# Two-layer decoder trunk on one core: VectorE in place of GpSimd for the two-operand SBUF arithmetic of layer 0's attention, with a new order of work

## The chip, the cores and the metric

The kernel runs on one core of a Trainium2 chip. A core has five engines that matter here: TensorE (PE in the profile; PEld is its weight load), VectorE (DVE), ScalarE (ACT), GpSimd (POOL) and SyncE (SP), which issues all transfers. Each engine works through its own list of instructions in order; semaphores hold an instruction back until what it reads is there. The metric is the device time of one launch in microseconds, lower is better.

## The reference, cut to what matters

`x` is 256 tokens by 1024 features in float32. Layer 0 is native sparse attention, layer 1 dilated window attention, each with a conditioned norm in front, an output projection, a gated residual add behind, and one norm at the end.

```
h = rms_norm(x, g) * (1 + scale) + shift            # shift, scale, gate: silu(c) @ w_ada + b_ada
u = h @ w_in                                        # q, k_c v_c k_s v_s k_w v_w, z, gate logits
k_cmp, v_cmp = compress(k_c), compress(v_c)         # 15 blocks of 32 tokens, two small matmuls each
o_cmp = softmax(q k_cmp) v_cmp
o_slc = softmax(rope(q) rope(k_s)) v_s              # 4 blocks of 64 tokens, top 16: all visible ones
o_win = softmax(rope(q) rope(k_w)) v_w              # window 512: all earlier tokens
o = g0 * o_cmp + g1 * o_slc + g2 * o_win
x = x + gate * ((o * silu(z)) @ w_out)
...                                                 # layer 1: 16 heads in three (window, dilation) groups
out = rms_norm(x)
```

## The kernel before, in words

Activations lie with tokens or features on the 128 partitions, always whole in SBUF. Weights stream in from memory once, in pieces of 256 KB to 512 KB (tile `raw`). Float32 products are made from a split: a weight piece `raw` is copied to a rounded `wh`, and the rest `wl = raw - wh` is computed (`split`, line 445); activations are split in the same way into `hH`/`hL` (in the attention `hl`, `kl`, and `a` for the operands of later products). A product of two split operands takes three matmuls, `wh*hH + wh*hL + wl*hH`. Every 128 x 512 weight piece so costs a copy and a subtraction before TensorE may use it, and both have two SBUF operands or one.

The program falls into stages, which the code calls phases: 0 the norm of layer 0 and the first part of its input projection, accumulated over 8 slices k of the features in eight banks of PSUM (`lin` three, `s` two, `o` and `t`); 1 the rest of that projection and the whole attention of layer 0; 2 its output projection; 3 and 4 layer 1's projections and attention, half the heads each; 5 layer 1's weighing of the groups, its z gate and its output projection.

In phase 1 there are, beside the matmuls: the splits of the weights that are left of `w_in`; rotary embedding (`rope`, line 696: products of PSUM with a table, then a sum of two SBUF tiles, `t1 + t2`); the splits of q and k (`q_stack`, `k_stack`); the sum with the position table and the probabilities of the compressed branch (`cmp_blocks`, `cmp_probs`); per pair of heads `pair0` (line 940): scores in PSUM, a masked maximum on VectorE (`pt<-pss,ct`), exponentials on ScalarE, a scaling of each 128-row piece of probabilities (`pt<-pt,sm`), transposes on TensorE (`pst<-ct,pt`), their copies to SBUF (`pT<-pst`) and the product with v (`pso<-pT,v`); and the gating of each pair by z and its split (`w<-w,a`, `a<-w,a`).

Nothing is issued in the order in which it is written. Each operation is recorded with its operands (`Order.add`, line 127) and with the engines that may run it: "SV" for a copy, "VG" or "GV" for a sum or difference, "GVS" for the scaling of probabilities. `Order.schedule` (line 193) then fixes one list for each engine: it walks through a planned time with a table of instruction costs, takes on each engine the operation that can start first, breaks ties by a priority (the place in the text plus the group's number in `SHIFT`), and hands an operation with a choice of engines to the one on which it would end first, the cost weighted by the table `W` (one number for each engine and phase). `EARLY` moves the transfers of a group forward or back in SyncE's list. All instructions are therefore issued from one line, 335, and the profile's groups are told apart by their tiles.

What the change touches is the rule in `add` (lines 157 to 164). In the phase whose number is `SPLIT`, an operation that VectorE may share with another engine loses VectorE if it has two wide SBUF operands (`two`) or is a copy or a scaling from SBUF to SBUF (`one`); otherwise it loses GpSimd. In every other phase a choice between VectorE and GpSimd always goes to VectorE. With `SPLIT = 1` the sums and differences of two SBUF tiles in phase 1 so run on GpSimd, the copies from SBUF to SBUF there on ScalarE, and the copies out of PSUM on VectorE or ScalarE.

## Time and profile before

| | us |
|---|---|
| median of 3 runs | 353.34 (350.19 to 354.21) |
| profiled execution, device time | 351.29 |
| its span, first to last instruction | 349.5 |
| TensorE busy | 331.9 (95%) |
| VectorE busy | 241.2 (69%), 699 instructions |
| ScalarE busy | 231.5 (66%) |
| GpSimd busy | 62.3 (18%), 79 instructions |

The span lies 1.8 us under the profiled execution's own time, which lies 2.05 us under the median. A matmul counts as busy from its start to a modelled end, and matmuls overlap, so TensorE's busy time is a cover of the span and not its load. A row of a timeline gives the start, the time covered, the engine, the operation with its tiles, and in brackets the idle time before it with the instruction that ended it. In groups, `x112 | 75.2, 708 | 30.9` is 112 instructions, 75.2 us covered by them, 708 ns the mean of one from start to end, and 30.9 us of idle time in front of them. Means are longer than busy time divided by the count, since the end of one instruction overlaps the start of the next.

### The profile page before, as it was taken

To read this page: it belongs to the slowest core of one execution; us is meant where nothing else is said; L and a number is where in the kernel's file an instruction comes from. 1 tells how busy PE (TensorE), PEld (TensorE's weight loads), DVE (VectorE), ACT (ScalarE), POOL (GpSimd) and SP (SyncE) were. 2 spreads that over 40 slices of the span, in tenths; PEclk is the share of its full clock that TensorE was granted. 3 is DMA by queue.
4 is the path that set the end of the run, shared out by engine and by line. 5 is a ranking of instruction groups with operands and counts; after the bars stand their busy time and mean duration, and the time that the engine had idled before them with its cause. 6 is when DMAs were issued, how large, how long until landed. Compare 5 with 4: busy or idle time off the path is not lost.

```text
span 349.5 us, 6498 instructions
## 1 busy us (share of the span) xinstructions
PE 331.9 (95%) x2217; PEld 264.5 (76%) x2217; DVE 241.2 (69%) x699; ACT 231.5 (66%) x618; POOL 62.3 (18%) x79
## 2 busy tenths in 40 slices
PE   8698999899999999999999799999999999999991
PEld 7485778787956688766886577787887889799881
DVE  1536255666987687868669799946788449597864
ACT  4736245575876998997348765787468788456614
POOL 1000000699721572015400200000000000000000
PEclk9998999999999999999999999999999999999997
DMA  7999996743979941618963974943556125145003
GB/s 234 338 362 355 351 360 190 203 154 102 380 245 356 383 166 62 241 39 317 361 221 106 338 245 121 342 150 113 181 179 190 53 81 167 56 127 175 1 0 120
DMA packets 45168, 71.35 MB, mean 204 GB/s; under 512 B 4712, under 2 KB 22352, under 8 KB 45136
## 3 DMA queue, kind: packets, MB, share of 16 engines
q1 hardware_dynamic: 45136, 70.94, 61.2%
q8 instruction: 17, 0.28, 0.3%
q14 instruction: 15, 0.12, 0.1%
HBM read 69.88 MB, written 1.05 MB: 203 GB/s over the span
## 4 chain that ended last, share of the span: by engine, by line
PE 78%; ACT 5%; DVE 4%; DMA 4%; POOL 4%; issue 2%; SPq 1%; ACTq 0%; POOLq 0%; DVEq 0%
PE pslin L335 50%; PE pst L335 13%; PE pss L335 9%; PE pso L335 6%; DMA raw<-in_nsa_w_in_dram 3%; ACT a L335 2%; DMA vec<-in_ada_b_dram 1%; ACT wh L335 1%; SPq L335 1%; POOL wl L335 1%; DVE t L335 1%; DVE a L335 1%; ACT w L335 1%; POOL sm L335 1%; DVE x L335 1%
## 5 line engine op out<-in xcount | busy, mean ns | idle before, releaser
L335 DVE TENSOR_TENSOR wl<-raw,wh 128x512 fp32r<-128x512 f32 (+2 forms) x128 | 82.5, 683 | 31.9 <-ACT wh L335 25.8
L335 ACT ACTIVATE wh<-raw 128x512 fp32r<-128x512 f32 (+3 forms) x144 | 78.3, 592 | 38.6 <-DMA raw<-in_nsa_w_in_dram 9.3
L335 PE MATMUL pslin<-wh,hH 128*128 128x512 f32 (+1 forms) x136 | 54.5, 405 | 3.1 <-ACT hH L335 3.1
L335 PE MATMUL pslin<-wl,hH 128*128 128x512 f32 (+1 forms) x136 | 53.9, 401 | 0.7 <-DVE wl L335 0.6
L335 PE MATMUL pslin<-wh,hL 128*128 128x512 f32 (+1 forms) x136 | 54.3, 400 | 0.0
L335 ACT ACTIVATE pt<-pt,sm 128x128 f32<-128x128 f32 (+1 forms) x128 | 51.3, 443 | 1.5 <-DVE sm L335 1.3
L335 DVE CUSTOM_DVE_ANT_0 pt<-pss,ct 128x256 f32<-128x256 f32 (+1 forms) x96 | 30.6, 351 | 12.3 <-PE pss L335 9.1
L335 POOL TENSOR_TENSOR sm<-sm,mhalf 128x1 f32<-128x1 f32 x6 | 4.9, 816 | 181.2 <-DVE sm L335 171.2
L335 POOL TENSOR_TENSOR wl<-raw,wh 128x256 fp32r<-128x256 f32 (+2 forms) x24 | 23.9, 1015 | 63.7 <-ACT wh L335 63.6
L335 PEld LDWEIGHTS pslin<-wh,hH 128*128 128x128 f32 x136 | 25.8, 191 | 9.5 <-ACT hH L335 3.7
L335 PE MATMUL pslin<-hH,wh 128*128 128x256 f32 x112 | 31.9, 290 | 1.1 <-DVE t L335 1.1
L335 PE MATMUL pslin<-hH,wl 128*128 128x256 f32 x112 | 31.1, 292 | 0.2 <-POOL wl L335 0.2
L335 PE MATMUL pslin<-hL,wh 128*128 128x256 f32 x112 | 31.1, 288 | 0.0
L335 PE MATMUL pslin<-wh,a 128*128 128x512 f32 x96 | 30.4, 396 | 0.0
L335 PEld LDWEIGHTS pslin<-wl,hH 128*128 128x128 f32 x136 | 25.9, 190 | 5.8 <-DVE wl L335 1.1
L335 PE MATMUL pss<-a,a 128*128 128x256 f32 (+2 forms) x128 | 30.0, 324 | 0.0
L335 PEld LDWEIGHTS pslin<-wh,hL 128*128 128x128 f32 x136 | 26.0, 191 | 4.9 <-issue 0.8
L335 PE MATMUL pst<-ct,pt 128*128 128x128 f32 x144 | 27.2, 280 | 0.0
L335 ACT ACTIVATE a<-pst 128x512 fp32r<-128x512 f32 (+5 forms) x37 | 20.1, 571 | 8.2 <-PE pst L335 8.0
L335 PEld LDWEIGHTS pss<-a,a 128*128 128x128 f32 x128 | 20.8, 190 | 3.0 <-DVE am L335 0.8
L335 PEld LDWEIGHTS pslin<-hH,wh 128*128 128x128 f32 x112 | 21.1, 189 | 2.0 <-ACT wh L335 1.4
L335 PEld LDWEIGHTS pst<-ct,pt 128*128 128x128 f32 x144 | 17.5, 141 | 6.6 <-ACT pt L335 2.0
(206 smaller groups left out, 658.2 us busy)
## 6 DMA issues: line engine op xcount, KB each, us to landing
raw<-in_ada_w_dram SPq DMA_DIRECT2D x32, 512.0 KB, 5.8
raw<-in_dil_w_in_dram SPq DMA_DIRECT2D x32, 512.0 KB, 4.4
a<-in_ada_w_dram SPq DMA_DIRECT2D x32, 256.0 KB, 5.3
raw<-in_nsa_w_in_dram SPq DMA_DIRECT2D x12, 384.0 KB, 4.5
raw<-in_nsa_w_out_dram SPq DMA_DIRECT2D x8, 512.0 KB, 4.9
raw<-in_dil_w_out_dram SPq DMA_DIRECT2D x8, 512.0 KB, 3.6
raw<-in_nsa_w_in_dram SPq DMA_DIRECT2D x8, 320.0 KB, 5.4
raw<-in_nsa_ck_w_dram SPq DMA_DIRECT2D x4, 512.0 KB, 5.4
```

The costliest lines, as they stand in the source:

```text
L335: getattr(self.eng[o["eng"]], name)(*map(self.bind, a), **{n: self.bind(x) for n, x in k.items()})
```

## The change

`SPLIT` becomes -1, which is no phase's number, so the rule of phase 1 is gone: sums and differences of two SBUF tiles go to VectorE in all phases, copies and scalings from SBUF to SBUF may go to VectorE or ScalarE in phase 1 as elsewhere. GpSimd keeps the six small powers of the norms and three fills with zero. `W`, all 62 entries of `SHIFT` and most of `EARLY` (47 entries before, 51 now) have new values, so that the lists of all engines are new in all phases.

```diff
     COLD = 6900.0
-    SPLIT = 1
+    SPLIT = -1
     SWITCH = 140.0
-    W = {"V": [28.3311, 11.5606, 58.1165, 39.0311, 46.0334, 38.3357], "S": [15.1009, 14.1134, 11.5755, 23.4489, 27.2999, 8.7042], "G": [22.0, 22.0, 22.0, 22.0, 22.0, 22.0]}
+    W = {"V": [34.4666, 16.9669, 58.5786, 53.4999, 34.5476, 45.0449], "S": [21.8443, 11.231, 8.2993, 26.6967, 27.0326, 28.6422], "G": [22.0, 22.0, 22.0, 22.0, 22.0, 22.0]}
...
```

By the lists of the two kernels, 66 sums, differences and products of phase 1 move from GpSimd to VectorE (14 of 128 x 512, 12 of 128 x 384, 28 of 128 x 256, 12 of 128 x 128). Over all phases 105 copies and scalings with an SBUF source move from ScalarE to VectorE (44 of them scalings of probabilities, 37 roundings `wh<-raw`), and 64 copies out of PSUM move from VectorE to ScalarE (29 of them `pT<-pst`): now all of `pT`, `qp`, `kl` and the transposed operands `a<-pst` are copied by ScalarE. VectorE's list grows from 699 to 806 instructions. TensorE has the same matmuls in another order.

Three places of the new lists follow; a tile's first number tells buffers of one name apart and its last number is given when it is placed, so the last numbers differ between the lists.

The first is VectorE's list where phase 0 ends and phase 1 begins: `pslin_14` and `pslin_15` hold the first 512 columns (q) of the projection for the two halves of the tokens, `t1_151` and `t2_152` are the rotary products of the first, `qp` and `a4_112` plain copies. Before:

```order
L335 TENSOR_TENSOR wl_103_1528<-raw_50_1366,wh_102_1520 128x512
L335 TENSOR_TENSOR wl_103_1528<-raw_50_1366,wh_102_1520 128x256
L335 COPY qp_115_1572<-pslin_14_1129 128x512
L335 TENSOR_TENSOR t1_151_1579<-pslin_14_1129,ct_68 128x512
L335 TENSOR_TENSOR t2_152_1587<-pslin_14_1129,ct_68 128x8x32
L335 COPY a4_112_1595<-pslin_16_1167 128x512
L335 COPY w1_114_1607<-pso_17_1177 128x128
L335 COPY a4_112_1595<-pso_17_1177 128x512
```

and now:

```order
L335 TENSOR_TENSOR wl_103_1528<-raw_50_1369,wh_102_1521 128x256
L335 TENSOR_TENSOR wl_103_1528<-raw_50_1369,wh_102_1521 128x512
L335 CAST wh_127_1542<-raw_123_1384 128x256
L335 TENSOR_TENSOR wl_128_1547<-raw_123_1384,wh_127_1542 128x256 x2
L335 CAST wh_129_1563<-raw_124_1411 128x256
L335 TENSOR_TENSOR wl_130_1567<-raw_124_1411,wh_129_1563 128x256 x2
L335 TENSOR_TENSOR t1_151_1575<-pslin_14_1128,ct_68 128x512
L335 TENSOR_TENSOR t2_152_1584<-pslin_14_1128,ct_68 128x8x32 x2
L335 TENSOR_TENSOR t1_157_1593<-pslin_15_1130,ct_68 128x512
```

The splits of the next weights (`wl_128`, `wl_130`) have come from GpSimd and stand in front of the rotary products; the plain copies out of PSUM are gone to ScalarE, so both second products `t2_152` follow at once and the bank `pslin_14` is read out sooner after its last matmul.

The second is TensorE's list at the same place: `pslin_163` is the first block of z columns (one `lin` bank, which it takes over from `pslin_14`), `pst_20` the last bank of the projection in phase 0. Before:

```order
L335 MATMUL pso_17_1177<-wl_101_1502,hH_87 128x432
L335 MATMUL pss_18_1189<-wh_102_1520,hH_87 128x512
...
L335 MATMUL pst_20_1204<-hH_87,wh_102_1520 128x256
L335 MATMUL pst_20_1204<-hL_88,wh_102_1520 128x256
L335 MATMUL pst_20_1204<-hH_87,wl_103_1528 128x256
L335 MATMUL pslin_163_1642<-hH_87,wh_127_1541 128x256
L335 MATMUL pslin_163_1642<-hL_88,wh_127_1541 128x256
```

and now:

```order
L335 MATMUL pso_17_1165<-wl_101_1511,hH_87 128x432
L335 MATMUL pslin_163_1598<-hH_87,wh_127_1542 128x256
L335 MATMUL pslin_163_1598<-hL_88,wh_127_1542 128x256
...
L335 MATMUL pslin_163_1598<-hH_87,wl_132_1617 128x256
L335 MATMUL pss_18_1179<-wh_102_1521,hH_87 128x512
L335 MATMUL pss_18_1179<-wh_102_1521,hL_88 128x512
```

The z block now begins before the last slice of the banks `s` and `t`, 18 of its matmuls ahead of them, where it stood behind all of them.

The third is ScalarE's list in phase 0 at the third slice k: `t2_69` is a copy on the way to the slice's scale and shift (`Acol`, `Bcol`), `w1_70` applies them, `hH_87` is what the matmuls wait for. Before:

```order
L335 ACTIVATE t2_69_1248<-pst_68_1233 128x512
L335 ACTIVATE wh_73_1253<-raw_32_1121 128x512
L335 ACTIVATE wh_73_1253<-raw_32_1121 128x256
L335 ACTIVATE wh_76_1267<-raw_33_1124 128x512
L335 ACTIVATE wh_76_1267<-raw_33_1124 128x432
L335 ACTIVATE w1_70_1284<-a4_7_1093,Bcol_86,Acol_85 128x256
L335 ACTIVATE w1_75_1290<-a4_7_1093,Bcol_86,Acol_85 128x256
L335 ACTIVATE hH_87<-w1_70_1284 128x256
```

and now:

```order
L335 ACTIVATE t2_69_1252<-pst_68_1237 128x512
L335 ACTIVATE wh_73_1259<-raw_32_1125 128x512
L335 ACTIVATE wh_76_1273<-raw_33_1132 128x512
L335 ACTIVATE wh_76_1273<-raw_33_1132 128x432
L335 ACTIVATE w1_70_1284<-a4_7_1100,Bcol_86,Acol_85 128x256
L335 ACTIVATE hH_87<-w1_70_1284 128x256
L335 ACTIVATE hH_87<-w1_75_1287 128x256
```

One rounding and the second slice's `w1_75` are on VectorE now, so `hH_87` follows `w1_70` directly.

## Rows read from the trace of the kernel before

**Rows 1.** The page, part 1: each engine's busy us, share, instructions.

```profile
PE 331.9 (95%) x2217; PEld 264.5 (76%) x2217; DVE 241.2 (69%) x699; ACT 231.5 (66%) x618; POOL 62.3 (18%) x79
```

**Rows 2.** Windows: stretch, its us; PE, PEld, DVE, ACT, POOL busy; clock; DMA.

```profile
30.00:40.00 10.00, 8.55 (x42) 6.43 (x46) 4.79 (x13) 4.29 (x10) 0.00 (x0) 0.83 1.07 359
...
200.00:210.00 10.00, 10.00 (x46) 7.87 (x45) 9.76 (x24) 6.66 (x16) 0.00 (x0) 1.00 0.77 256
...
60.00:100.00 40.00, 38.53 (x275) 31.96 (x274) 29.73 (x95) 26.98 (x82) 31.10 (x41) 1.00 0.61 201
100.00:165.00 65.00, 64.09 (x575) 47.76 (x575) 49.80 (x206) 57.36 (x190) 21.32 (x23) 1.00 0.67 231
...
200.00:340.00 140.00, 140.00 (x862) 115.78 (x861) 105.20 (x266) 91.72 (x222) 0.03 (x1) 1.00 0.43 139
```

**Rows 3.** What TensorE waited for: us in total, times, longest.

```profile
PE pslin L335 <- ACT hH L335: 3.1, 2, 1.7
PE pslin L335 <- DVE t L335: 2.7, 3, 1.1
...
PE pslin L335 <- POOL wl L335: 0.2, 1, 0.2
```

**Rows 4.** TensorE's timeline at its longest waits after 30 us.

```profile
32.15 1.22 PE L335 MATMUL pslin<-wh,hH 128*128 128x512 f32 x2 [1.45 <-ACT hH L335]
...
68.92 0.36 PE L335 MATMUL pslin<-hH,wh 128*128 128x256 f32 x1 [1.10 <-DVE t L335]
...
163.34 0.83 PE L335 MATMUL pslin<-selc,t 128*128 128x1 f32 x6 [0.55 <-DVE t L335]
...
193.75 0.51 PE L335 MATMUL pslin<-wl,hH 128*128 128x512 f32 x1 [0.65 <-DVE wl L335]
...
198.05 0.66 PE L335 MATMUL pst<-ct,a 128*128 128x128 f32 x4 [1.23 <-ACT a L335]
```

**Rows 5.** Groups by shape: GpSimd's large ones, then VectorE's of like shapes.

```profile
L335 POOL TENSOR_TENSOR wl<-raw,wh 128x512 fp32r<-128x512 f32 x8 | 10.2, 1285 | 11.5 <-ACT wh L335 11.4
...
L335 POOL TENSOR_TENSOR wl<-raw,wh 128x256 fp32r<-128x256 f32 x8 | 5.8, 743 | 52.1 <-ACT wh L335 52.1
...
L335 DVE TENSOR_TENSOR wl<-raw,wh 128x512 fp32r<-128x512 f32 x112 | 75.2, 708 | 30.9 <-ACT wh L335 25.1 <-DMA a<-in_ada_w_dram 3.6 <-PE pslin L335 1.7
...
L335 DVE TENSOR_TENSOR hL<-w,hH 128x128 fp32r<-128x128 f32 x16 | 3.6, 284 | 0.0
L335 DVE TENSOR_TENSOR wl<-raw,wh 128x256 fp32r<-128x256 f32 x8 | 3.3, 418 | 0.0
...
L335 DVE TENSOR_TENSOR t<-pslin,ct 128x384 f32<-128x384 f32 x2 | 1.1, 550 | 0.0
```

**Rows 6.** Timeline from 161 to 168 us: VectorE's subtractions, then one of GpSimd's.

```profile
161.45 1.24 DVE L335 TENSOR_TENSOR wl<-raw,wh 128x512 fp32r<-128x512 f32 x1 [0.82 <-ACT wh L335]
...
166.61 4.72 DVE L335 TENSOR_TENSOR wl<-raw,wh 128x512 fp32r<-128x512 f32 x5
...
166.64 1.25 POOL L335 TENSOR_TENSOR w<-w,a 128x256 f32<-128x256 f32 x1
```

**Rows 7.** Groups by shape that ScalarE and VectorE exchange.

```profile
L335 ACT ACTIVATE wh<-raw 128x512 fp32r<-128x512 f32 x115 | 66.9, 623 | 34.6 <-DMA raw<-in_nsa_w_in_dram 9.3 <-PE pslin L335 7.5 <-DMA raw<-in_nsa_w_out_dram 7.1
L335 ACT ACTIVATE pt<-pt,sm 128x256 f32<-128x256 f32 x64 | 29.7, 496 | 0.9 <-DVE sm L335 0.8
...
L335 DVE COPY pT<-pst 128x512 f32<-128x512 f32 x15 | 10.2, 689 | 2.3 <-PE pst L335 2.1
...
L335 DVE CAST wh<-raw 128x512 fp32r<-128x512 f32 x5 | 2.1, 426 | 4.2 <-PE pslin L335 4.2
```

**Rows 8.** Timeline, single instructions that move or are moved past.

```profile
30.70 1.09 ACT L335 ACTIVATE w<-a,Bcol,Acol 128x256 f32<-128x256 f32 x2
...
63.87 0.69 DVE L335 COPY qp<-pslin 128x512 f32<-128x512 f32 x1 [3.82 <-PE pslin L335]
...
345.18 1.33 ACT L335 ACTIVATE a<-a,sm 128x512 f32<-128x512 f32 x2 [0.98 <-POOL sm L335]
```

More of the change, by code (lines that the diff above doesn't have):

```diff
@@ L407, in trunk_kernel @@
     WINDOW = {"a4": 12, "hl4": 16, "kl": 1, "qp": 1, "t1": 4, "t2": 6, "pT": 3, "pt": 1, "raw": 4, "wh": 4, "wl": 16, "w1": 6, "sm": 8, "lin": 16, "s": 3, "t": 16, "o": 8}
-    SHIFT = {"alpha": 89017, "att1": 61585, "att10": 35605, "att11": 19738, "att12": -8457, "att13": 30069, "att14": -56182, "att15": 14273, "att16": -83050, "att17": -72423, "cmp": 3663, "cmp1": -23102, "cmp2": 28835, "cmp3": 7460, "cmp4": -48216, "gate1": 72239, "gate10": -85627, "gate11": -51363, "gated0": 149938, "gated00": 4110, "gated01": -5470, "gated02": 26781, "gated03": 93383, "gemv": 26274, "gemv0": -40566, "gemv1": 73921, "gemv2": 119153, "gemv3": 89366, "gemv4": 132954, "gemv5": 22317, "head": -123025, "out0": -60938, "out1": 2775, "pair": -129487, "pair0": 22859, "pair1": 99414, "pair2": -125283, "pair3": -104240, "pair4": 28914, "pair5": -83279, "pair6": -9286, "pair7": 66257, "qkv1": 68172, "qkv10": 32210, "qkv11": -107202, "qkv12": 37053, "qkv13": 8324, "qkv14": -34818, "qkv15": 131303, "rest": 7469, "warm": 121005, "z0": -122337, "z0b": 56550, "z1": 50917, "z10": -58693, "z11": -10741, "z12": 24741, "z13": 59833, "z14": 209247, "z15": -32118, "z16": -111480, "z17": -11407}
@@ L409, in trunk_kernel @@
-    EARLY = {"alpha": -230, "att1": 169, "att11": 82, "att13": -195, "att14": 55, "att15": -96, "att16": -4, "att17": -369, "cmp": 517, "cmp1": -418, "cmp2": -421, "cmp3": 299, "gate1": -190, "gate10": -129, "gate11": -412, "gated0": -35, "gated00": 47, "gated01": -405, "gated02": -146, "gemv0": -174, "gemv1": -251, "gemv2": -25, "gemv5": -658, "head": -175, "out0": -35, "out1": -17, "pair1": 223, "pair4": -14, "pair5": -31, "pair6": 45, "pair7": -58, "qkv1": -37, "qkv10": 93, "qkv12": -4, "qkv13": 22, "qkv14": 102, "qkv15": -300, "rest": -370, "warm": 145, "z0": 78, "z1": -92, "z11": 284, "z13": -98, "z14": 31, "z15": -157, "z16": 57, "z17": 190}
+    SHIFT = {"alpha": 90989, "att1": 68590, "att10": 91628, "att11": 54221, "att12": 23576, "att13": 85967, "att14": -25086, "att15": 38798, "att16": 20174, "att17": -51605, "cmp": -43589, "cmp1": -118184, "cmp2": -41242, "cmp3": 10076, "cmp4": -70993, "gate1": 119363, "gate10": -87187, "gate11": -54365, "gated0": 112320, "gated00": -66144, "gated01": 10287, "gated02": -67254, "gated03": 118277, "gemv": 42475, "gemv0": -51946, "gemv1": 17289, "gemv2": 182855, "gemv3": 112428, "gemv4": 70080, "gemv5": 32963, "head": -83420, "out0": -59234, "out1": 40336, "pair": -142736, "pair0": 69985, "pair1": 143639, "pair2": -115306, "pair3": -125796, "pair4": 50600, "pair5": -104767, "pair6": 27161, "pair7": 73490, "qkv1": 114280, "qkv10": -9872, "qkv11": -141163, "qkv12": -12274, "qkv13": -16812, "qkv14": -18443, "qkv15": 89967, "rest": 11362, "warm": 140924, "z0": -91650, "z0b": 24129, "z1": 27901, "z10": 27309, "z11": -4958, "z12": 59455, "z13": 63980, "z14": 177237, "z15": -6409, "z16": -1446, "z17": 13711}
@@ new lines, in trunk_kernel @@
+    EARLY = {"alpha": 11, "att11": 13, "att12": -11, "att13": -133, "att14": -48, "att15": 153, "cmp": 555, "cmp1": -489, "cmp2": -440, "cmp3": 148, "gate1": -146, "gate10": 175, "gate11": -419, "gated0": 37, "gated00": -75, "gated01": 22, "gated02": 18, "gated03": -149, "gemv": 65, "gemv0": -405, "gemv1": -260, "gemv2": 83, "gemv3": -211, "gemv4": 150, "gemv5": -788, "head": -478, "out0": 16, "out1": 241, "pair": 594, "pair1": 77, "pair2": 5, "pair3": -316, "pair4": 1027, "pair5": -4, "pair6": 30, "pair7": 80, "qkv1": -7, "qkv11": 2, "qkv12": 82, "qkv13": -319, "qkv14": 34, "rest": -40, "warm": -296, "z0": -48, "z0b": 186, "z1": -20, "z10": 65, "z11": 20, "z14": -138, "z15": 171, "z16": 5}
```

## The prediction

> **What bounds the kernel now.** The page's first part comes first: TensorE covers 95% of the span, VectorE 69%, ScalarE 66%, GpSimd 18% [rows 1]. Then the windows, because these shares are means over stages that differ. In 200 to 340 us TensorE is busy for all of 140 us, and VectorE at 9.76 of 10 us in one slice there does not hold it back [rows 2]. In 60 to 100 us, where the attention of layer 0 begins, TensorE is covered for 38.5 of 40 us, VectorE for 29.7, ScalarE for 27.0 and GpSimd for 31.1; in 100 to 165 us TensorE for 64.1 of 65, GpSimd for 21.3 [rows 2]. So GpSimd's work fills much of one stage, and TensorE hardly waits there. The list of waits agrees: TensorE waited 0.2 us for a GpSimd subtraction in the whole run [rows 3]. The reader is to see that TensorE's matmuls are the bound, and that the matmuls are the same after the change. What can move is the few microseconds that TensorE stands idle, and they lie at five places [rows 4].
>
> **What the change moves.** GpSimd's 66 large instructions take 57.8 us by their groups, 1285 ns for one of 128 x 512 and 743 for 128 x 256 [rows 5]. On VectorE I price a piece by busy time over count: 75.2/112 = 0.67 us for 512 columns, 0.55 for 384, 3.3/8 = 0.41 for 256, 3.6/16 = 0.225 for 128 [rows 5]. That makes 14 x 0.67 + 12 x 0.55 + 28 x 0.41 + 12 x 0.225 = 30 us of new work for VectorE. The exchange with ScalarE is nearly even on VectorE: 64 copies out of PSUM go (0.68 us for 512 columns), 105 roundings and scalings from SBUF come (2.1/5 = 0.42 us for 512 columns; ScalarE takes 623 ns, and 496 for a scaling of 256) [rows 7]. By their sizes I put both at 34 to 37 us. VectorE so goes from 241 to about 270 us, 77% of the span. Nothing of this is on the path by itself. What counts is each place where TensorE waits or may come to wait, in order of time:
>
> 1. **The third slice of phase 0.** TensorE waits 1.45 us for `hH` [rows 4]. ScalarE did two `w` in 1.09 us before the first `hH` [rows 8]; now one of the two is on VectorE and a rounding ahead of them too. I take half of the pair, -0.6 us; ends 0 (VectorE delays the scale and shift in front of it as much) and -1.45.
>
> 2. **The clock.** In 30 to 40 us the granted clock averages 0.83 [rows 2], which is 3.4 us at the lower level of 1.2 GHz, 1.7 us of work lost, during and after that wait. TensorE's new list still runs dry there, so I leave it: 0, with ends -1.7 (no fall) and +1.7 (one more elsewhere).
>
> 3. **The hand-over to phase 1.** TensorE waits 1.10 us for the rotary product that reads out the bank which the z block needs [rows 4]. By the new list of VectorE the copies are gone from between the two products, and the weight splits ahead of them (two of 256 rounded, four subtracted, about 2.3 us) fit into the 3.82 us that VectorE was idle before its first copy at 63.87 [rows 8]. Eighteen matmuls of the z block also stand ahead of the last slice of the banks `s` and `t` now, so that this slice covers what comes late. I take -1.0; ends -1.1 and +0.5 (`wl_132`, which TensorE wants twelve short matmuls later, is now behind `t1_157` on VectorE).
>
> 4. **VectorE in 60 to 100 us.** GpSimd's 39 large instructions of this window (10 of 256, 6 of 512, 11 of 384, 12 of 128 columns) are 16.9 us on VectorE at the prices above. The copies out of PSUM that leave it are 15 x 0.68 + 2.7 = 12.9 us; roundings and scalings that come are about 4.6. So 29.7 + 16.9 - 12.9 + 4.6 = 38.3 of 40 us: VectorE is as long here as TensorE. Queued behind its splits of weights are the rotary sums, q's split and the masked maxima, each of which TensorE waits for in turn. Lower end 0: the slice 200 to 210 us shows VectorE at 9.76 with TensorE full [rows 2]. Upper end +6: before, VectorE was idle 40 - 29.7 = 10.3 us, waiting for results; 2.3 of it is filled by step 3, and if the other 8 stay, 46.3 us are needed. I take +1.5, a quarter of the way, nearer to the row at 9.76.
>
> 5. **The start of the output projection, 161 to 170 us.** Here GpSimd's gating overlaps VectorE's `wl`, and these take 1.24 us, and five together 4.72 us, where five at 0.67 would be 3.4; GpSimd's own pieces take 1.25 in place of 0.74 [rows 6, 5]. So 0.6 + 1.3 = 1.9 us come back on VectorE; the last eight products and subtractions at 0.41 us put 3.3 on it. TensorE's wait here is 0.55 us behind the first slow `wl` [rows 4]. I take 0; ends -0.55 and +1.4.
>
> 6. **The norm before layer 1.** TensorE waits 0.65 and 1.23 us [rows 4]. In the new lists the second half of x is updated at once after its product with the gate, where eleven others stood between, but its transposes stand 11 matmuls behind the first of layer 1 and not 20. I take 0; ends -1.9 and +1.9.
>
> 7. **Layer 1.** TensorE has no idle time to give [rows 2]; the new lists move about 9 us from ScalarE to VectorE (105 to 114 of 140). I take +0.5; ends 0 and +3.
>
> 8. **The end.** The last scaling, two pieces of 1.33 us together on ScalarE [rows 8], is now one piece on each engine: -0.3, ends 0 and -0.6, since SyncE issues the two transfers one after the other anyway.
>
> **The sum** is -0.6 + 0 - 1.0 + 1.5 + 0 + 0 + 0.5 - 0.3 = +0.1 us, 351.4 against the profiled execution's 351.29. The median of the runs shown lies 2.05 us above that execution, so I forecast **353.4 us: no change** that a measurement can tell (about 1%, 3.5 us).
>
> **The rivals.**
>
> *Faster: the waits at the hand-overs go.* Steps 1, 3, 5, 6 and 8 at their good ends, -0.6 - 1.1 - 0.55 - 1.9 - 0.6, and nothing lost in 4 and 7, give 351.3 - 4.8 = 346.5, as a median 348.6; with the clock of step 2, 346.9. For it: GpSimd's pieces are nearly twice as long as VectorE's, and chains of splits get shorter. Against it: TensorE waited 0.2 us for GpSimd [rows 3], and each of these places has its own delay on ScalarE or VectorE. Chance 0.21. The Trainium skill, "GPSIMD Engine Reference", section Specifications, says that GpSimd shares its SBUF interfaces with VectorE and contends with instructions of VectorE that read two SBUF inputs. The trace shows that in step 5 alone, since the rule of line 157 kept such instructions off VectorE elsewhere in the phase; if VectorE set the end there, its 1.9 us would give a median of 351.5, still no change.
>
> *Slower: VectorE becomes the bound where the attention begins.* The place is 60 to 100 us, the price up to the +6 of step 4 in place of 1.5: 351.4 + 4.5 = 355.9, as a median 358.0. It decides the sign once VectorE keeps more than 6.7 of its 8 us of waiting, so that TensorE loses 5. For it: 38.3 of 40 us, in a stage whose VectorE instructions wait for TensorE and ScalarE by turns. Against it: TensorE has matmuls of the remaining projection to run in between, and the rows at 9.76. Chance 0.22. The Trainium skill, "Perfetto Trace Analysis", section Optimizing Scalar/DVE Operations, speaks for this way: where VectorE is saturated, giving work to ScalarE or even GpSimd may make sense, and the change does the reverse; it adds that VectorE and GpSimd share a read port, so that such offloading might not help. By the first half the sum has the +6, by the second it has 0; no row before shows VectorE saturated together with a TensorE that waits.
>
> *The exchange with ScalarE matters more than GpSimd.* The change says GpSimd, but the 64 copies out of PSUM that go to ScalarE are in front of more matmuls. In 100 to 165 us ScalarE is busy for 57.4 of 65 us [rows 2], and it now alone empties PSUM. For it: every `pT` stands on that engine, behind its exponentials. Against it: 44 scalings leave it. At 1.5 us in layer 0 and 2 in layer 1, 351.4 + 3 = 354.4, as a median 356.5: within 1%, with a tail beyond. Chance 0.15, of which 0.04 slower by over 1%.
>
> **Range and chances.** My forecast has 0.42; its own bounds, with the clock, reach from 350 to 356. The range of 347.5 to 358.5 takes in the faster rival down to all but its clock gain and the slower one to its price; I leave out some 0.1 on each side. Faster by over 1% (below 349.8): 0.21. Slower (above 356.9): 0.22 + 0.04 = 0.26. Within 1%: 0.53.
>
> **What would show it.** Step 4: VectorE above 36 of 40 us in 60 to 100, and TensorE's waits for `t`, `hl` or `pt` there under 3 us in all; over 5 means the slower rival. Step 3: no wait of a microsecond at the first z matmul. Step 1: `hH` of the third slice half a microsecond earlier. Step 5: `wl` at 0.7 us throughout, and VectorE full from 160 to 170. Step 7: TensorE still covered for 139 us or more of layer 1's 140. I am wrong if TensorE's total of waits after 30 us moves by more than 4 us, or if its covered time itself moves, which would mean that the order of matmuls costs something that I count as nothing: changes between kinds of matmul are about as many in both lists, 296 and 304.

## The result, and the profile after

The changed kernel takes 350.53 us (median of 20 executions, 349.08 to 355.4), the kernel before 352.79 (20 executions, 350.19 to 354.5): a ratio of 0.9945, 95% interval 0.9927 to 0.9964. That is 2 us, or 0.55%, faster. The forecast was 353.4 and no change; the time lies in its range of 347.5 to 358.5, and the gain is under 1%, but its interval excludes no change.

The execution profiled for the changed kernel has a span of 350.9 us, 1.4 more than the one of before, because its clock fell twice and that of before once (below). So stretches are compared, not the two ends. Each engine's busy us, share and instructions, against [rows 1]:

```profile
PE 336.4 (96%) x2217; PEld 266.7 (76%) x2217; DVE 261.1 (74%) x806; ACT 215.0 (61%) x577; POOL 4.4 (1%) x13
```

Windows, against [rows 2] (busy us of PE, PEld, DVE, ACT, POOL; clock; DMA):

```profile
10.00:20.00 10.00, 7.79 (x61) 5.49 (x59) 6.82 (x20) 6.28 (x13) 0.55 (x1) 0.83 1.05 332
30.00:40.00 10.00, 8.39 (x42) 7.08 (x39) 5.14 (x14) 5.32 (x11) 0.00 (x0) 0.83 1.03 353
60.00:100.00 40.00, 39.65 (x278) 31.82 (x280) 35.88 (x130) 29.61 (x85) 0.31 (x2) 1.00 0.73 236
70.00:80.00 10.00, 10.00 (x77) 9.62 (x76) 10.00 (x31) 8.39 (x21) 0.00 (x0) 1.00 0.38 112
100.00:165.00 65.00, 64.44 (x574) 47.82 (x570) 52.60 (x240) 53.71 (x179) 0.00 (x0) 1.00 0.54 187
...
200.00:340.00 140.00, 139.90 (x860) 116.28 (x859) 111.82 (x284) 79.57 (x200) 0.00 (x0) 1.00 0.44 144
```

VectorE is busy for 35.9 of 40 us where the attention begins, and for 10.00 of 10 in one slice of it, and TensorE is covered for 10.00 there too. The waits that [rows 4] showed have these lines in TensorE's timeline now (start, covered us, idle time before with what ended it):

```profile
33.58 1.22 PE L335 MATMUL pslin<-wh,hH 128*128 128x512 f32 x3 [1.61 <-ACT hH L335]
...
67.60 0.36 PE L335 MATMUL pslin<-hH,wh 128*128 128x256 f32 x1 [0.29 <-DVE t L335]
...
194.37 0.49 PE L335 MATMUL pslin<-wh,hH 128*128 128x512 f32 x1 [0.91 <-ACT hH L335]
```

The third slice waits as before, 1.61 against 1.45. The z block waits 0.29 instead of 1.10. At 162 us no wait above 0.25 is left: the copy `t<-pslin` that TensorE waited for there stood behind VectorE's slow subtraction of [rows 6], and ScalarE does it now. The line of before, then that of the changed kernel:

```profile
162.61 0.68 DVE L335 COPY t<-pslin 128x512 f32<-128x512 f32 x1
```

```profile
160.48 0.60 ACT L335 ACTIVATE t<-pslin 128x512 f32<-128x512 f32 x1 [1.40 <-PE pslin L335]
```

The norm before layer 1 has one wait of 0.91 in place of 0.65 and 1.23. The wait of 1.23 hung on one of the small powers that GpSimd keeps: it took 2.13 us in the kernel before, beside VectorE's subtractions, and 0.55 in the changed one, where VectorE runs none of them then. Three lines of before, then one of the changed kernel:

```profile
194.94 1.89 DVE L335 TENSOR_TENSOR wl<-raw,wh 128x512 fp32r<-128x512 f32 x3
195.11 2.13 POOL L335 TENSOR_TENSOR sm<-sm,mhalf 128x1 f32<-128x1 f32 x1 [8.81 <-DVE sm L335]
197.28 1.34 ACT L335 ACTIVATE a<-x,sm 128x512 f32<-128x512 f32 x2 [2.01 <-POOL sm L335]
```

```profile
193.82 0.55 POOL L335 TENSOR_TENSOR sm<-sm,mhalf 128x1 f32<-128x1 f32 x1 [3.42 <-DVE sm L335]
```

The two durations are the same in all seven traces of the kernel before, with and without the additions below, and in the three of the changed one. VectorE's subtractions at the start of the output projection, against [rows 6]:

```profile
165.47 0.69 DVE L335 TENSOR_TENSOR wl<-raw,wh 128x512 fp32r<-128x512 f32 x1 [0.31 <-ACT wh L335]
...
168.56 1.89 DVE L335 TENSOR_TENSOR wl<-raw,wh 128x512 fp32r<-128x512 f32 x3
```

They take 0.69 and 0.63 us each, where they took 1.24 and 0.94 beside GpSimd. One wait that shrank is at a place that the prediction did not list, the first slice of phase 0. In a second execution of the changed kernel, and in the profiled one of before (TensorE's timeline, in this order):

```profile
16.78 0.50 PE L335 MATMUL pslin<-wh,hH 128*128 128x512 f32 x1 [1.10 <-DVE hH L335]
```

```profile
16.49 0.73 PE L335 MATMUL pslin<-wh,hH 128*128 128x512 f32 x2 [1.69 <-ACT hH L335]
```

Before, ScalarE did a copy of 0.59 us between `w` and its rounding `hH`; now VectorE rounds, in 0.30 us. That this gains time is not shown: the slice begins at 16.5 to 17.1 us in four executions of the kernel before and at 15.9 to 17.7 in three of the changed one.

### The profile page after: what moved, and what is told of

Read it like the earlier page. It is cut to its first block, busy times and chain, and to the rows that moved or that the text cites. A ratio compares the mean times of both kernels' runs of the same rounds, so it can differ in the third digit from the quotient of the medians.

```text
span 350.9 us, 6460 instructions
## 1 busy us (share of the span) xinstructions
PE 336.4 (96%) x2217; PEld 266.7 (76%) x2217; DVE 261.1 (74%) x806; ACT 215.0 (61%) x577; POOL 4.4 (1%) x13
## 4 chain that ended last, share of the span: by engine, by line
PE 76%; DMA 10%; DVE 7%; ACT 3%; SPq 1%; issue 1%; POOL 0%; POOLq 0%; ACTq 0%
PE pslin L335 47%; PE pst L335 13%; PE pss L335 9%; PE pso L335 6%; DMA raw<-in_nsa_w_out_dram 5%; DMA raw<-in_nsa_w_in_dram 3%; DVE wl L335 2%; DMA vec<-in_ada_b_dram 2%; SPq L335 1%; DVE pt L335 1%; ACT wh L335 1%; DVE t L335 1%; ACT a L335 1%; DVE x L335 1%; DVE sm L335 1%
## 5 line engine op out<-in xcount | busy, mean ns | idle before, releaser
L335 DVE TENSOR_TENSOR wl<-raw,wh 128x512 fp32r<-128x512 f32 (+3 forms) x152 | 92.7, 646 | 26.2 <-ACT wh L335 23.5
L335 ACT ACTIVATE wh<-raw 128x512 fp32r<-128x512 f32 (+3 forms) x107 | 59.8, 600 | 52.6 <-PE pslin L335 18.6
L335 ACT ACTIVATE pt<-pt,sm 128x128 f32<-128x128 f32 (+1 forms) x84 | 36.3, 444 | 5.5 <-DVE sm L335 5.4
L335 ACT ACTIVATE a<-pst 128x512 fp32r<-128x512 f32 (+5 forms) x49 | 26.3, 558 | 6.5 <-PE pst L335 6.0
L335 ACT ACTIVATE pT<-pst 128x256 f32<-128x256 f32 (+1 forms) x48 | 22.5, 484 | 3.1 <-PE pst L335 2.6
L335 PEld LDWEIGHTS pslin<-hH,wl 128*128 128x128 f32 x112 | 20.7, 188 | 1.2 <-DVE am L335 0.4
```

The lines of the kernel that those rows point to most:

```text
L335: getattr(self.eng[o["eng"]], name)(*map(self.bind, a), **{n: self.bind(x) for n, x in k.items()})
```

## The experiments

Medians are in us. Each kernel was timed beside the kernel before, whose median was 352.6 to 353.2 each time.

### Are the falls of the clock the difference?

First the kernel before again, twelve executions, and then single profiled executions of both kernels.

> The kernel before, unchanged, for the spread of its clock. If falls of the granted clock in 10 to 20 and in 30 to 40 us come by chance and not with one of the two kernels, its executions show mean clocks of 0.98 to 0.997 like those of the changed kernel, about 1.7 us of span for each fall, and the profile shows one or two of them; if they belong to its order of work, every execution has the one fall of 30 to 40 us and none in 10 to 20, and its spans agree within 0.5 us.

> The kernel before, unchanged, one execution with its profile. The medians differ by 2.2 us, but from 60 us on the two traces at hand differ by only 0.2 us. Theory F (falls of the clock): executions of the kernel before have a fall more than those of the changed one, in the first 80 us, each with up to 1.7 us; this execution shows one or two such falls and lies above 351 us where they cover matmuls. Theory D (transfers and waits in phase 0): the falls are as many in both kernels, and the difference lies in the time of the first 60 us without them.

> The changed kernel, unchanged, one execution with its profile. Theory F: one fall at most that covers matmuls, and a time of 349.5 to 351. Theory D: falls as in the kernel before, and less time in the first 60 us beside them.

> The kernel before once more, as in the first look. Theory F: falls that cost 1.7 us or more in all, above 351 us. Theory D: no more falls than the changed kernel's looks show.

> The changed kernel once more, as in its first look. Theory F: one fall at most that covers matmuls, 349.5 to 351 us. Theory D: falls as in the kernel before, and the difference in the waits of the first 60 us.

The kernel before again took 352.26 (ratio 0.9993, 0.9963 to 1.0022), 349.98 to 355.68. Its profiled execution (350.4) had no fall before its last matmul. The single executions of the kernel before took 355.72 and 351.99, those of the changed one 352.2 and 350.5. Windows of the first and longest, then of the second of the changed kernel:

```profile
10.00:20.00 10.00, 6.31 (x55) 3.73 (x55) 5.32 (x16) 7.74 (x17) 0.55 (x1) 0.92 1.10 338
20.00:30.00 10.00, 10.00 (x44) 8.47 (x43) 3.52 (x8) 3.20 (x7) 0.00 (x0) 0.73 1.06 358
30.00:40.00 10.00, 8.55 (x47) 6.15 (x47) 4.15 (x11) 4.99 (x12) 0.00 (x0) 0.83 1.08 363
```

```profile
10.00:20.00 10.00, 7.63 (x67) 5.19 (x66) 6.74 (x20) 7.24 (x16) 0.55 (x1) 1.00 1.10 343
20.00:30.00 10.00, 10.00 (x62) 7.35 (x61) 3.87 (x10) 3.83 (x8) 0.00 (x0) 1.00 1.04 348
30.00:40.00 10.00, 8.40 (x40) 6.51 (x43) 5.56 (x15) 3.84 (x9) 0.00 (x0) 0.83 1.05 358
```

The clock column is the mean of the two levels, so 0.83 of 10 us is 1.7 us lost, and the first of them lost 0.8 + 2.7 + 1.7 = 5.2. By this sum the four profiled executions of the kernel before lost 1.7, 0, 5.2 and 1.7 us, the three of the changed one 3.4, 1.7 and 1.7. All these falls lie in phase 0, and they come by chance. Otherwise executions of one kernel agree closely: of the intervals from one start of a matmul to the next after 60 us, only four differ by over 0.15 us among the four executions before, seven among the three of the changed kernel.

Then TensorE got something to do in these waits: products of zeros, placed before five matmuls of phase 0, every other instruction where it was.

```diff
+            for _ in range(self.FILL.pop(o["mark"], 0) if o["eng"] == "PE" else 0):
+                to, go = self.bind(...), o["calls"]["PE"][0][2].get("start", True)
+                self.eng["PE"].matmul(to[:, 0:...], self.zero[:, ...], self.ident[:, 0:...], start=go, stop=go, ...)
             for name, a, k in o["calls"][o["eng"]]:
```

> The kernel before with all its lists, and 18 matmuls of zeros (128 columns, about 0.22 us each) on TensorE in the waits of phase 0: 2 before the transpose of vec, 1 before the first scale and shift, 2 before the second half of x, 7 before the first slice, 6 before the third. Theory F (the granted clock falls after TensorE has stood idle there, by chance, and costs 1.7 us each time): no fall before the last matmul, executions closer together, and a median of 350.0 to 351.0, near the 350.4 of the one execution without a fall. Theory D (the falls do not hang on these waits, the differences are transfers): falls as before, median 352 to 354.

> The changed kernel with all its lists, and 16 such matmuls of zeros in its own waits of phase 0 (3, 1, 1, 4 and 7 at the same five places). Theory F: no fall, a median of 348.8 to 349.6, and 0.6 to 1.3 us less than the kernel before with its filled waits, in place of 2.2: the rest of the change's gain is falls that no longer happen. Theory D: 350 to 351.5, and still 2 us less than the kernel before with filled waits.

The kernel before took 351.66 so (351.03 to 353.02; ratio 0.9987, 0.9964 to 1.001), the changed kernel 349.46 (348.87 to 350.75; ratio 0.9932, 0.9909 to 0.9954). No fall is left before the last matmul, here in windows of the filled kernel before:

```profile
10.00:20.00 10.00, 9.04 (x85) 7.07 (x84) 5.58 (x17) 8.31 (x18) 0.56 (x1) 1.00 1.11 338
...
30.00:40.00 10.00, 9.89 (x64) 7.19 (x64) 5.12 (x13) 4.62 (x11) 0.00 (x0) 1.00 1.06 362
```

Both medians are a little over a microsecond lower than without filling, which for the kernel before its interval does not tell from nothing. 2.2 us still lie between the two, where theory F asked for 0.6 to 1.3.

Yet these are not the same 2.2 us. The span and the mean granted clock were noted for every execution, and the span times one minus the clock is the time lost at the lower clock, the idle end of the kernel included (1.4 to 2.7 us of it by the traces). So counted, the kernel before lost 4.4 us (mean of 107 executions) and the changed kernel 3.3 (its 20): a difference of 1.1 us, 95% interval by resampling 0.3 to 1.8, and 1.0 us (0.6 to 1.4) is left between their times when it is taken off. With filled waits the lost times differ by only 0.4 us, and 1.9 us (1.5 to 2.3) are left, because the rest of the kernel before is 1.2 us longer when it is filled; its traces show two new waits of that size together (below). So fewer or shorter falls are, by these counts, about half of what the change gains without filling, though seven traces are too few to show it and the executions were not all taken side by side. The filled changed kernel has the lowest median of all that ran, under both kernels.

### Is it the engine, or the order?

Two kernels kept all lists of TensorE, ScalarE and SyncE and exchanged engines alone; in a third the planner set all lists anew with the old numbers. The edit of the first, at the place where an operation is issued (`swap` holds VectorE's form of GpSimd's operation):

```diff
-            for name, a, k in o["calls"][o["eng"]]:
-                getattr(self.eng[o["eng"]], name)(...)
+            for name, a, k in o["swap"] if o["swap"] and o["eng"] == "G" else o["calls"][o["eng"]]:
+                getattr(self.eng["V" if o["swap"] and o["eng"] == "G" else o["eng"]], name)(...)
```

> The kernel before with its numbers and all of its lists for TensorE, ScalarE and SyncE; only the 66 sums, differences and products of phase 1 that GpSimd ran are issued on VectorE, at the places that their planned starts give them in its list. Theory A (the engine itself is worth the gain, VectorE has room): VectorE goes from 241 to about 271 us, TensorE's waits at 68.9 and 163 us shrink, 0.5 to 2 us faster than before. Theory B (the room is made by the copies that ScalarE takes over in the change): 60 to 100 us then asks 29.7 + 16.9 = 46.6 of 40 us from VectorE, TensorE waits for it there, 4 to 8 us slower than before.

The second does the reverse, with `swap = [calls["G"]]` for the same 66 in the changed kernel; the third is one line.

```diff
-    SPLIT = 1
+    SPLIT = -1
```

> The changed kernel with its numbers and all of its lists for TensorE, ScalarE and SyncE; only the 66 two-operand instructions of phase 1 are issued on GpSimd instead of VectorE. Theory A (VectorE's shorter instruction is what gains): GpSimd's 1.29 us for 128 x 512 in place of 0.67 makes TensorE wait again where a split or a gating is the last to come; 2 to 6 us slower than the changed kernel. Theory C (the new order gains, whatever engine does the sums): within 0.7 us of the changed kernel's 350.5, VectorE at about 19 of 40 us in 60 to 100.

> The kernel before with its old priorities and weights, and only SPLIT = -1: the planner itself puts the sums on VectorE and moves copies between VectorE and ScalarE as its costs say, and all lists are planned anew. Theory A: within 1 us of the changed kernel (350 to 351.5), since the engine makes the gain. Theory C (the new numbers make it): slower than before by 1 to 6 us, because the old numbers were found for the old rule.

| | us | ratio to before (95%) |
|---|---|---|
| kernel before, the 66 on VectorE | 362.25 | 1.028 (1.0242 to 1.0317) |
| changed kernel, the 66 on GpSimd | 357.42 | 1.014 (1.0106 to 1.0175) |
| kernel before with `SPLIT = -1` alone | 382.39 | 1.0826 (1.0775 to 1.0878) |

VectorE in place of GpSimd costs the old order 9.5 us; GpSimd in place of VectorE costs the new order 6.9. Theory B of the first and theory A of the second had the sign, and both costs lie above their ranges (8 and 6 us). The old numbers with the new rule cost 29.7 us, five times what theory C had at most. In these two orders neither engine is the better one by itself: each order is made for its division of the work. The windows of the first of the three:

```profile
60.00:100.00 40.00, 35.86 (x224) 29.66 (x223) 35.47 (x107) 21.60 (x62) 0.31 (x2) 0.96 0.58 192
100.00:165.00 65.00, 61.82 (x537) 45.48 (x539) 56.85 (x227) 54.25 (x185) 0.00 (x0) 1.00 0.58 196
```

VectorE is busy for 35.5 of 40 us there, as in the changed kernel (35.9), and yet TensorE is covered for 35.9 only and not for 39.7 (a fall of the clock, 1.7 us, lies in this window too). The busy share of VectorE does not tell the two apart; what stands in front of what in its list does. TensorE waited 2.39 us for a rotary product at the z block there.

Next, the division of work nearly as in the change, at the old order, and the change with one part of the division undone.

```diff
+                swap = {"G" if two else "S": ("V", calls.pop("V"))}
+                swap = swap if two or "vpt_" in outs[0].tensor.name else {}
...
+        if self.phase == 1 and psum and "S" in calls:
+            swap["V"] = ("S", calls["S"])
```

> The kernel before with its numbers and its lists for TensorE and SyncE; in phase 1 the 66 instructions of GpSimd are issued on VectorE, and in exchange the 64 copies out of PSUM that VectorE ran on ScalarE and the 64 scalings of probabilities that ScalarE ran on VectorE, nearly the change's division of work at the old order. Theory E (the division makes the gain): 350 to 351.5. Theory O (the new order of TensorE's list and of the others is needed for it): slower than before by 1 to 6 us, though less than the 9.5 us that the sums alone cost, with waits of TensorE for VectorE or ScalarE in 60 to 100 us.

```diff
+        swap = [calls["V"]] if self.phase == 1 and psum and "S" in calls and "pT" in outs[0].tensor.name else None
```

> The changed kernel with all its other lists; the 32 copies pT<-pst of phase 1 go back from ScalarE to VectorE, 16 x 0.68 + 16 x 0.4 = 17 us of work that VectorE has to do in addition in 70 to 165 us. Theory S (VectorE has slack there, TensorE runs other matmuls meanwhile, as the charge of +1.5 that did not come suggests): within 1 us of the changed kernel. Theory B (the exchange with ScalarE is what keeps VectorE off the path: 88.5 of 105 us in 60 to 165 becomes full): 3 to 8 us slower than the changed kernel, TensorE waiting for pT and pt.

The first took 362.67 (1.0302, 1.0251 to 1.0352), no better than the sums alone, so theory E fell and O held, though its price was above the 6 us that it gave. The second took 358.97 (1.0205, 1.0173 to 1.0238), 8.4 us over the changed kernel: theory B, a little above its range. Windows of the second:

```profile
60.00:100.00 40.00, 39.23 (x281) 30.48 (x283) 36.43 (x131) 28.66 (x83) 0.31 (x2) 1.00 0.71 230
100.00:165.00 65.00, 60.24 (x511) 44.96 (x507) 59.70 (x251) 41.58 (x145) 0.00 (x0) 1.00 0.48 163
```

Between 100 and 165 us VectorE is at 59.7 of 65 (52.6 in the changed kernel) and TensorE loses 4.2 us of cover there. The rival in which VectorE becomes the bound is a real mechanism; the copies out of PSUM that ScalarE takes over keep it away.

### Which piece gains?

On the filled changed kernel (349.46), one piece at a time was put back: an operation of these tiles went to VectorE (the first) or to GpSimd (the other two), at the place that it had.

```diff
+        swap = [calls["V"]] if ... outs[0].tensor.name.startswith(("vqp_115_", "va4_112_", "vw1_114_")) else None
...
+        swap = [calls["G"]] if self.phase == 1 and "G" in calls and names[0] == "vwl" else None
...
+        swap = [calls["G"]] if ... names[1:] in (["vw1", "va4"], ["va4", "vw1"]) else None
```

> The changed kernel with matmuls of zeros in the waits of phase 0 (median 349.46 by itself), and four copies out of PSUM at the hand-over to phase 1 (qp, two of a4, w1) back from ScalarE to VectorE, where the kernel before had them. Theory H (step 3: these copies in front of the rotary products hold the bank that the z block needs): TensorE waits 0.9 to 1.4 us instead of 0.3 at the first z matmul after 64 us, the end 0.5 to 1.0 us later. Rival (TensorE's own new order there, 18 z matmuls ahead of the last slice, makes the gain): wait within 0.2 us of 0.3, the end within 0.3 us.

> The changed kernel with filled waits, and of the two-operand instructions only the 24 weight splits wl<-raw,wh of phase 1 on GpSimd. All 66 together cost 6.9 us there. Theory W (what TensorE waits for on GpSimd are the splits of the remaining projection): 4 us slower or more. Rival (it is the sums on the way to q, k and the scores, rotary sums, hl and kl): under 2 us slower.

> The changed kernel with filled waits, and of the two-operand instructions only the 12 of the gating (w<-w,a and a<-w,a, 128 x 256) on GpSimd. Theory G (GpSimd beside VectorE's weight splits slows both and delays the start of the output projection): wl takes 1.1 to 1.3 us there instead of 0.67, TensorE waits 0.5 us or more, 0.5 to 1.5 us slower than 349.46. Rival (the gating has time, its engine does not matter): within 0.3 us.

For the fourth, the entries of layer 1's groups (`qkv1`, `att1`, `gate1`, `z1` with their numbers, `alpha`, `out1`) in `SHIFT` and `EARLY` and the last three numbers of each row of `W` are those of the kernel before:

```diff
-    W = {"V": [34.4666, 16.9669, 58.5786, 53.4999, 34.5476, 45.0449], "S": [21.8443, 11.231, 8.2993, 26.6967, 27.0326, 28.6422], ...}
+    W = {"V": [34.4666, 16.9669, 58.5786, 39.0311, 46.0334, 38.3357], "S": [21.8443, 11.231, 8.2993, 23.4489, 27.2999, 8.7042], ...}
```

> The changed kernel with filled waits, and for layer 1 alone (its groups in SHIFT and EARLY and the weights of phases 3 to 5) the numbers of the kernel before; nothing changes up to 170 us. Theory N (the new order gains in layer 1 and at the norm before it): TensorE waits 1.88 us at the norm as before instead of 0.9, and the end is 0.5 to 1.5 us later. Rival (the waits taken away at the norm come back as short stalls between matmuls, layer 1 as a whole neither gains nor loses): the time from 170 us to the end within 0.4 us.

**The hand-over.** 350.93 (349.92 to 352.24), 1.5 us more; by the traces 1.2. TensorE's timeline:

```profile
64.78 0.36 PE L340 MATMUL pslin<-hH,wh 128*128 128x256 f32 x1 [0.52 <-DVE t L340]
67.60 0.38 PE L340 MATMUL pslin<-hH,wl 128*128 128x256 f32 x1 [0.72 <-DVE wl L340]
```

The wait for the rotary product grows from 0.30 to 0.52, and a new one comes after it, for a weight split that stands behind the copies: 1.24 us in all at this place, theory H, though the larger half of it is not at the first z matmul. **The splits.** 354.59 (353.73 to 355.57), 5.1 us more: 24 of the 66 instructions make most of the 6.9, as theory W had it. **The gating.** 350.04 (348.98 to 351.95), 0.6 us more by the medians, which lies in theory G's range, and 0.2 by the traces, which lies in the rival's; twelve executions with a spread of 3 us do not decide between them. GpSimd's and VectorE's timelines in it:

```profile
162.81 0.74 POOL L340 TENSOR_TENSOR a<-w,a 128x256 fp32r<-128x256 f32 x1 [0.41 <-DVE a L340]
164.97 1.27 POOL L340 TENSOR_TENSOR a<-w,a 128x256 fp32r<-128x256 f32 x1 [1.41 <-ACT a L340]
```

```profile
162.97 1.13 DVE L340 TENSOR_TENSOR wl<-raw,wh 128x512 fp32r<-128x512 f32 x1 [0.23 <-ACT wh L340]
...
164.36 3.64 DVE L340 TENSOR_TENSOR wl<-raw,wh 128x512 fp32r<-128x512 f32 x5
```

Both engines are slowed where they meet (1.27 against 0.74, 1.13 against 0.69), as in [rows 6], and in the trace TensorE does not wait for it: of theory G the first half holds.

**Layer 1.** 356.77 (356.22 to 357.89), 7.3 us more, of which 3.4 are time at the lower clock by the trace, and neither theory: the mixed numbers delay a transfer of the output projection's weights, ScalarE's rounding waits for it, and TensorE for that, before layer 1 has begun.

```profile
171.29 2.08 PE L338 MATMUL pslin<-wh,a 128*128 128x512 f32 x4 [4.90 <-ACT wh L338]
...
198.23 0.50 PE L338 MATMUL pslin<-wl,hH 128*128 128x512 f32 x1 [0.64 <-DVE wl L338]
...
202.52 0.66 PE L338 MATMUL pst<-ct,a 128*128 128x128 f32 x4 [1.23 <-ACT a L338]
```

Its time is of no use for the question, but its last two lines are: with the old numbers of layer 1 alone the two waits of the norm are back, 0.64 and 1.23, as in [rows 4], and GpSimd's power there takes 2.13 us again.

Then the hand-over was tried the other way round, in the filled kernel before, and that kernel was run once more.

```diff
+        swap = [calls["S"]] if "S" in calls and outs[0].tensor.name.startswith(("vqp_115_", "va4_112_", "vw1_114_")) else None
```

> The kernel before with GpSimd's work unchanged and with filled waits in phase 0 (median 351.66 by itself), and only the four copies at the hand-over (qp, two of a4, w1) issued on ScalarE instead of VectorE. Theory H (these four copies are the 1.3 us that putting them back cost the changed kernel, and GpSimd has no part in it): TensorE's wait of 1.10 us at the first z matmul falls to 0.5 or less, and the end comes 0.6 to 1.1 us earlier, 350.5 to 351.0. Rival (the place was made by the sums that left GpSimd and by TensorE's new order; ScalarE's copies now delay the next roundings wh): wait 0.9 us or more in all at the z block, the end within 0.3 us or later.

> The kernel before with filled waits once more, for a second trace. The first showed an execution of 351.0, 0.65 us under its kernel's median, and the traces account for some 0.9 of the 2.2 us between the kernels. Theory V (the kernel before has waits for transfers that come in some executions only, as 0.5 us each at two places from 110 to 120 us): the rows from 100 us on differ from those of the first by 0.5 us or more in few places. Rival (nothing varies after the phase 0): the rows agree within 0.2 us and the difference lies ahead of the first slice.

Moving only the four copies made it no faster: 352.25 (351.91 to 355.15) against 351.87 (351.21 to 353.16) for the same kernel without the move. TensorE's line, then VectorE's (the rest of its rotary products begin at 68.61):

```profile
69.17 0.36 PE L339 MATMUL pslin<-hH,wh 128*128 128x256 f32 x1 [1.83 <-DVE t L339]
```

```profile
64.02 1.02 DVE L339 TENSOR_TENSOR t<-pslin,ct 128x512 f32<-128x512 f32 x2 [4.45 <-ACT qp L339]
67.22 0.42 DVE L339 COPY v<-pss 128x256 f32<-128x256 f32 x1 [2.17 <-ACT w L339]
...
68.61 0.42 DVE L339 TENSOR_TENSOR t<-pslin,ct 128x256 f32<-128x256 f32 x1
```

VectorE stands idle for 2.17 us, because the next entry of its old list is a copy out of the bank `pss`, which waits for ScalarE, and the products that TensorE waits for stand behind it. In the changed kernel all four products follow each other (VectorE's timeline of the changed kernel):

```profile
66.10 1.95 DVE L335 TENSOR_TENSOR t<-pslin,ct 128x512 f32<-128x512 f32 x4 [0.28 <-ACT qp L335]
```

So theory H holds in the new order and not in the old one. The second trace of the filled kernel before shows waits like those of its first, of 0.46 and 0.61 us, at two places that none of the four executions without filling had at this size:

```profile
113.63 0.64 PE L338 MATMUL pss<-raw,a 128*32 128x256 f32 x8 [0.76 <-DMA raw<-in_nsa_cv_w_dram]
...
120.09 0.41 PE L338 MATMUL pst<-ct,pt 128*128 128x128 f32 x2 [0.62 <-ACT wh L338]
```

The first is a transfer of weights that lands later. The wait of 0.6 is in all three traces of the filled kernel before, with the four copies moved or not, so it comes with the filling; why was not found.

## Why the prediction was wrong

The forecast summed losses of 2.0 us (steps 4 and 7) against gains of 1.9 (steps 1, 3 and 8), and put three steps at 0. What failed are these zeros. **Step 6** put the norm's waits of 1.88 us at 0, and 0.97 of them went. **Step 5** put a wait of 0.55 at 0, and it went. **Step 2** put the clock at 0, and by the clocks of all executions 1.1 us went (0.3 to 1.8). Of the gains that it counted only that of step 3 came; steps 1 and 8 gave nothing. The losses were right in size, 1.6 us, but by luck: they came in another place and in another form than forecast.

How much was gained and lost behind phase 0 is best read from the first matmul of the eighth slice (62.97 us in the first trace of the kernel before) to the last matmul of the kernel, since both kernels have the same 1866 matmuls from there. This takes 278.9 to 279.4 us in four executions of the kernel before and 278.3 to 279.4 in three of the changed one, 0.3 less in the mean. All gaps in TensorE's cover sum to 4.1 to 4.3 us there before and to 2.3 after, 1.9 less. Against that, the intervals from one start of a matmul to the next, gaps taken off, grow by 1.6 us: by 1.9 up to layer 1, and they shrink by 0.3 in it. It is a little in many kinds: the output projection's 48 products `pslin<-wh,a` go from 11.2 to 11.8 us, the norm's 16 transposes `pst<-ct,a` from 1.42 to 1.92, the 64 `pso<-pT,v` of one half from 3.49 to 3.83. With filled waits the gaps are 5.1 and 5.4 against 2.0, 3.2 us less, the intervals again 1.6 longer, and 1.7 us are gained. The prediction counted the order of the matmuls as free and named a covered time that moves as what would prove it wrong; this is that, at 1.6 us. Ahead of the eighth slice, falls taken off, the means differ by another 0.3 us, but executions of one kernel differ by 0.6 to 0.9.

1. **Third slice:** forecast -0.6, measured +0.16 of waiting. The chain itself did get shorter as forecast: from the end of the small products with `selc` to the first matmul it took 2.15 us before (30.00 to 32.15) and takes 1.61 now (31.97 to 33.58). But before, five matmuls stood behind those products and covered part of it; in the new list nothing does. At the first slice the wait went from 1.69 to 1.10, and to 0.65 in the execution profiled first.
2. **Clock:** forecast 0 with 1.7 either way. The seven traces show falls in both kernels, but by the clocks of all executions the changed kernel loses 1.1 us less, inside the bounds and half of the gain. The reason given for the 0, that TensorE's list still runs dry at the third slice, is right (1.61 us) and did not settle it.
3. **Hand-over:** forecast -1.0; the wait went from 1.10 to 0.29, and four copies put back cost 1.2 to 1.5. Right. That ScalarE's taking the copies is the reason was half of it: without VectorE's new order it brings nothing.
4. **VectorE in 60 to 100 us:** forecast 38.3 of 40 us busy and +1.5; it is 35.9, and TensorE's waits of over 0.25 us for `t`, `hl` or `pt` there are the one of 0.29, where under 3 was asked. A loss exists, but as the longer intervals up to layer 1 (the 1.9 us above) and not as waits here; that VectorE causes them was not tested. The Trainium skill, "Perfetto Trace Analysis", section Optimizing Scalar/DVE Operations, says that a saturated VectorE may give work away to ScalarE. The trace agrees where the list leaves no room (32 copies given back to a VectorE at 52.6 of 65 us cost 8.4 us) and does not where TensorE has other matmuls meanwhile (VectorE at 10.00 of 10 us, TensorE covered for 10.00).
5. **Output projection:** forecast 0 and `wl` at 0.7 us; `wl` is at 0.69 and the wait of 0.55 is gone. GpSimd beside VectorE does slow both. Putting the gating back cost 0.2 us by the traces, but there ScalarE keeps the copy `t<-pslin`; in the kernel before this copy stood behind a subtraction of 1.24 us in place of 0.69, a difference as long as the wait. That the slowing made the wait is argued from the rows, and no run tests it alone. The Trainium skill, "GPSIMD Engine Reference", section Specifications, names the contention, and the rows agree (1.27 against 0.74 us, 1.13 against 0.69). The prediction saw it in step 5 alone; the trace of before shows it at the norm too (step 6).
6. **Norm before layer 1:** forecast 0, measured -0.97 of waiting (1.88 to 0.91). Two moves were named that were to offset each other. The first, the earlier update of x, worked as said (0.73 us after its product with the gate begins, in place of 3.17), and the second, transposes only eleven matmuls behind layer 1's first, cost nothing, because a third came that the step left out: GpSimd's power, 2.13 us beside VectorE's subtractions, takes 0.55. The 1.6 us saved there are more than the wait of 1.23 that is gone; this is read from the rows, and no run moves the power alone. What is new, the 0.91, stands in front of layer 1's first matmul: the first half's eight transposes came within the output projection before (187.46 and 188.13 us) and now come right ahead of that matmul (192.37).
7. **Layer 1:** forecast +0.5; TensorE is covered for 139.9 of 140 us, as asked. From layer 1's first matmul to the last of the kernel it takes 151.2 to 151.8 us in six executions before and 148.9 to 149.8 in four after, for the same 910 matmuls; without the norm's 1.88 us, which lie in it before, some 0.2 us remain as a gain. No loss of 0.5 came.
8. **The end:** forecast -0.3, measured 0: 7.30 us from the last matmul to the end in both. The last scaling ends 0.6 us sooner after the last matmul, and what lies behind it, with the last transfers, gives that back.

**Rivals.** *Faster*, 348.6, is what happened, at about half its size: the waits at the hand-overs shrank, and longer intervals took back half (filled) to five sixths (not filled) of the gaps that went. *Slower* did not happen, but three kernels (the 66 on VectorE at the old order, the same with the copies exchanged, and `pT` back on VectorE) showed that it waits close by. In the third rival, ScalarE does empty PSUM alone now, and it is busier only in 60 to 100 us, where it had room (29.6 of 40 us against 27.0); in 100 to 165 us it has less to do (53.7 of 65 against 57.4).

**What stays open.** By the time of the last matmul, falls taken off as above, the traces without filling account for some 0.6 us between the kernels (means of four and three executions), at the low end of the 1.0 (0.6 to 1.4) that the clocks of all executions leave; those with filling account for 1.8 and 2.2, where the medians say 2.2. Why the kernel before loses more time at the lower clock was not found. Nor was the old rule tried with numbers newly searched for it. So what is shown is that this order and this division of work gain together, and not that the exchange of engines is what gains: a better order for the old division may have done as much.

## What to carry to other kernels

Do not put a wait that the profile shows at a hand-over at 0 only because its bounds are even: of the 3.5 us in steps 3, 5 and 6, 2.3 went. Ask of each what it hangs on, down to the smallest instruction of the chain, and what will be late next; the third slice, where another engine was given half of the work, gained nothing. An engine's busy share does not tell whether it holds TensorE back: 35.5 and 35.9 of 40 us on VectorE were 9.5 us slower and 2 us faster. And one engine for another is not a change by itself: under a planner it is a new order, and the same exchange at the old order cost 9.5 us.

## What was not expected of the hardware

The granted clock fell in executions of an unchanged kernel from none to three times' worth (0 to 5.2 us lost) after waits of at most 1.7 us, and by chance; with products of zeros in these waits no profiled execution showed one in phase 0. GpSimd's 128 x 256 subtraction `a<-w,a` took 0.74 us alone and 1.27 beside VectorE's `wl`, which went from 0.69 to 1.13 us, and in that trace TensorE did not feel it. A power of one column on GpSimd took 0.55 us where none of these subtractions ran beside it and 2.13 beside three of them, and ScalarE and then TensorE waited for it. And a VectorE busy for 10.00 of 10 us, with TensorE at 10.00, was no sign of a bound.
